# A four-layer trunk on one core: the seven block products stepped singly, their first weight blocks loaded a block ahead, and x scaled on VectorE

## The chip, the core and the metric

The kernel runs on one core of a Trainium2 chip. The metric is the time of one execution in microseconds on the device; smaller is better. Three runs of the kernel before gave 1944.89, 1944.83 and 1941.6 us, median 1944.83. Engines are named as in the profile: PE is TensorE, with PEld for its weight loads, DVE is VectorE, ACT is ScalarE, POOL is GpSimd, and SP is the SyncE queue that issues nearly all DMAs.

## What is computed

```python
for i in range(4):                    # x is (1, 256, 1024) float32, D_FF = 2816
    x = x + 0.5 * swiglu(rms_norm(x, g[i,0]), gate[i,0], up[i,0], down[i,0])
    hn = rms_norm(x, g[i,1])
    x = x + (short_conv, mla, spatial_gating)[i % 3](hn)
    x = x + 0.5 * swiglu(rms_norm(x, g[i,2]), gate[i,1], up[i,1], down[i,1])

def swiglu(x, w_gate, w_up, w_down):
    return (silu(x @ w_gate) * (x @ w_up)) @ w_down
```

So there are twelve blocks in a row: feed-forward, mixer, feed-forward, four times over, all in float32. The 256 rows of x are two tiles of 128 rows.

## The kernel before

**Products.** A float32 operand is split into a high part of a rounded type (`whi`, made by ACT, line 111) and the rest (`wlo`, made by DVE, line 117). Each product is three matmuls: high by high (L327), high by low (L328), low by high (L330). The weights come in units of 512 KB: SP loads one into a `raw` buffer, ACT and DVE split it, PE uses it for both tiles. `Weights.get` makes up to AHEAD = 4 units ahead of the one in use; N_RAW = 5 raw buffers bound how far the loads run ahead.

**Turns.** The program is written out in one order, by two generators, one per tile. `advance(t)` takes a tile one turn further, which is usually six matmuls, and then runs what `later(n, ...)` has put off by n turns. Tile 0 leads by LAG = 4 turns; in a feed-forward block it is closed up to 1 turn (`follow`). Every engine executes its own instructions in this order, so an instruction that waits holds all that stand behind it on its engine.

**The seven products.** In each feed-forward block but the first, columns 2048 to 2559 of gate and of up are computed by Winograd's form of the 2x2 block product: the two tiles' rows and the two halves of the inner dimension are the blocks, and seven products of 128x512 by 512x256 replace eight. `sevens` is a third generator, the lane. Its first four half-steps make the sums s1 to s4 of the left blocks (`combine`, L603, on DVE; `high`, L608, on ACT; `low`, L613, on DVE), then come the right blocks' first form and, for each of two times seven products, a half-step that prepares and one that issues twelve matmuls (L744). `beside` grants the lane RATE = 0.6 half-steps a turn. Its credit grows from the turn on which the lane is set up, half-steps are taken only when all four halves of x are ready as left operands (`lhs`), and the `while` then takes as many as the credit covers. The four weight blocks of the gate unit (512 KB each, five buffers) are loaded when the lane is set up.

**x between blocks.** When half an x tile (512 columns) has its residual added (L418 or L420, DVE), `prepare_x` turns it over for the next block. Ahead of a feed-forward block with seven products it is `evened` first: ACT multiplies it by the last row scale (L436). Then either PE transposes it (L293), or DVE transposes 32x32 blocks (L455) and a DMA write (`xturn`, L461) and four reads (L465) do the rest, with raw loads held back between write and read. X_TAKE turns after the residual, ACT applies the gains (`take`, L441) and the half is split into high (L285, ACT) and low (L286, DVE).

Of the kernel before, what the change touches and what calls it, by code (L numbers as in the profile page):

```python
# [13 lines left out]
F32 = mybir.dt.float32  # L14
# [3 lines left out]
AF = mybir.ActivationFunctionType  # L18
# [22 lines left out]
N_UNITS = 9  # L41
N_RAW = 5
N_SEVENS_RAW = 5
N_SLOTS = 27
N_BIG = 4
# [116 lines left out]
def program(nc, pools, order, x, positions, norm_g, ffn_gate, ffn_up, ffn_down,  # L162
# [192 lines left out]
    def rows_into_x(t, a, m, ks, tail, factor, then):  # L355

        ps = [acc(), acc()]
        cols = [slice(0, 512), slice(512, 1024)]  # L360
        for n, k in enumerate(ks[: len(ks) - tail]):
            products(ps, a(k), k % 4, unit(t, m, k, 1, 0, D), 0, cols, n == 0, False)
            yield
        for h in range(2):
            for n in range(len(ks) - tail, len(ks), 2):
                k = ks[n]
                w = unit(t, m, k, 2, 512 * h, 512)
                for j in range(2):
                    products([ps[h]], a(k + j), (k + j) % 4, w, j, [cols[0]], n + j == 0, n + j == len(ks) - 1)
                if n < len(ks) - 2:  # L370
                    yield
            residual(t, ps[h], h, factor)
            if then is not None:
                prepare_x(t, h, *then)
            else:
                (nc.sync, nc.scalar)[h].dma_start(out=out[0, t * P : (t + 1) * P, 512 * h : 512 * h + 512], in_=x_half(t, h))
            if h == 0:
                yield
        in_chain[t] = True
# [45 lines left out]

    def prepare_x(t, h, i, which, halves_by_dma, evened):

# [3 lines left out]
        lhs[t][h] = None  # L431
        src = [x_half(t, h)]

        def even():
            src[0] = slot([P, 512])
            nc.scalar.activation(src[0], x_half(t, h), AF.Copy, scale=scales[t][0])  # L436

# [7 lines left out]
        if evened:  # L445
            even()
        if halves_by_dma[h]:
            later(evened, lambda: turn_half(src[0], take, X_TAKE - evened))
        else:
            later(X_TURN + evened, lambda: turn_by_pe(t, h, g, src[0]))  # L450

# [48 lines left out]
    def ffn(t, i, j, shared, then):  # L500
# [5 lines left out]
        if t == NT - 1 and seven:  # L506
            lanes.append(sevens(i, j, seven, shared))
        gate, up, down = (("gate", i, j), ("up", i, j), ("down", i, j))
# [31 lines left out]
        def body():  # L540
            yield from linear_group(t, a, [(gate, 0, lambda ps: gate_done(0, ps)), (up, 0, lambda ps: up_done(0, ps)),
                                           (gate, 512, lambda ps: gate_done(1, ps))], 512, NK)
            for n in plain[1:]:
# [4 lines left out]
                up_done(n, (yield from linear(t, a, up, c, w, NK)))  # L548
                yield
            yield from rows_into_x(t, lambda k: hs[k // 4], down, ks, tail, 0.5, then)  # L550

# [28 lines left out]

    def sevens(i, j, chunks, shared):

        (a11, a12), (a21, a22) = lhs[0], lhs[1]
        units = [(m, FF_CHUNKS[n][0]) for n in chunks for m in ("gate", "up")]
        raws = [{} for _ in units]

        def load(u, name_):
            if u == len(units):
                return
            m, c0 = units[u]  # L590
            row, col = int(name_[0]) - 1, int(name_[1]) - 1
            view = matrices[m][i, j].rearrange("(kt p) n -> p kt n", p=P)[:, 4 * row : 4 * row + 4, c0 + 256 * col : c0 + 256 * col + 256]
            raws[u][name_] = sevens_pool.tile([P, 4, 256], F32, tag="block", name=name("block"))
            nc.sync.dma_start(out=raws[u][name_], in_=view)

        for block in ("11", "12", "22", "21"):
            load(0, block)

# [108 lines left out]
        for s in range(last + 1):  # L707
# [4 lines left out]
            sum_of(s + 2)  # L712
            if (s + 1) % 7 == 4:
                load(u + 1, "12")
            if (s + 1) % 7 == 5:
                load(u + 1, "22")
                load(u + 1, "21")
            if q == 1:
                load(u + 1, "11")
            if pending:  # L720
# [39 lines left out]
    def conv(t, i, ia, shared, then):  # L760
# [44 lines left out]
        parts = ((c_done, D), (h_done, 2 * D), (b_done, 0))  # L805
        yield from linear_group(t, a, [(w_in, c, lambda ps, f=f: f(0, ps)) for f, c in parts], 512, NK)
        for f, c in parts:
            f(1, (yield from linear(t, a, w_in, c + 512, 512, NK)))
            yield
        yield from rows_into_x(t, lambda k: ms[k // 4], ("conv_out", ia), range(NK), OUT_TAIL, 1.0, then)  # L810


    sg_wT = [fixed([P, 4, P], f"sg_wT{j}") for j in range(2)]
    sg_gain = []

    def prepare_spatial(ic):
# [15 lines left out]
        def turn_over(j, wm):  # L832
            tr = transposed([wm[:, k, :] for k in range(4)])
            nc.scalar.activation(sg_wT[j], tr, AF.Copy)

        later(70, load)

    def spatial(t, i, ic, _, then):
# [47 lines left out]

        w_in = ("sg_in", ic)
        yield from linear_group(t, a, [(w_in, D, v_done), (w_in, D + 512, v_done), (w_in, 0, lambda ps: u_done(0, ps))], 512, NK)
        u_done(1, (yield from linear(t, a, w_in, 512, 512, NK)))
# [131 lines left out]
    def mla(t, i, ib, shared, then):  # L1021
# [164 lines left out]
        def finish(b8, o):  # L1186
            os_[b8] = lhs_of(o.rearrange("p h d -> p (h d)"), 4)

        for h0 in range(0, HEADS, per):
            p = scores(h0)  # L1190
# [47 lines left out]

    def beside():
        credit[0] += RATE  # L1240
        while lanes and credit[0] >= 1 and all(half_ is not None for tile_ in lhs for half_ in tile_):
            credit[0] -= 1
# [39 lines left out]
```

## Time and profile before

| | |
|---|---|
| profiled execution, its own time | 1946.05 us |
| its span | 1944.3 us |
| median of three runs | 1944.83 us |
| busy: PE, DVE, ACT, POOL | 95%, 66%, 52%, 7% of the span |
| mean granted TensorE clock | 0.978 |
| DMA | 400.36 MB, mean 206 GB/s |

Busy time of PE covers the time in which at least one matmul is in flight. The granted clock is 1.00 at TensorE's upper level, 2.4 GHz, and 0.50 at the lower, 1.2 GHz; in a stretch at 0.50 PE is busy and yet does half the work. The seven lanes start near 319, 516, 814, 1009, 1285, 1480 and 1772 us of the span.

### The profile page before, as it was taken

Reading aid. Unit: us, or ns where it says so; the run is one execution under the profiler, and the core shown is the slowest. Engines: PE = TensorE matmul, PEld = TensorE weight load, DVE = VectorE, ACT = ScalarE, POOL = GpSimd, SP = SyncE. Lnnn points to the kernel's source line nnn. Section 1 sums busy time; section 2 is a strip of 40 time slices with the busy share of each in tenths; the row PEclk is TensorE's granted clock in tenths of the full one; section 3 lists DMA queues with packets and bytes.
Section 4 is the critical chain, followed back from the end, with each engine's and each line's share of the span. In section 5 each row is a group of like instructions: output and inputs, shape, how many; then the busy total and the mean of one; then the engine's idle time right before and its main releaser. Section 6 shows DMA issues by size and latency. Waiting matters only on the chain.

```text
span 1944.3 us, 24911 instructions
## 1 busy us (share of the span) xinstructions
PE 1854.1 (95%) x9022; PEld 1535.9 (79%) x9022; DVE 1280.7 (66%) x1560; ACT 1009.3 (52%) x1447; POOL 131.9 (7%) x263
## 2 busy tenths in 40 slices
PE   8999998999799979899989998989998999998999
PEld 7888787887688868688868886868876887787887
DVE  5565677765577576686658664677656765667763
ACT  5344545545554485554455445565455544545542
POOL 2000101000600140100010101100000000000000
PEclk9999998999899999999999999989998999998999
DMA  7687656687667841666876786566876687656684
GB/s 242 225 238 223 211 177 213 196 239 221 196 211 216 241 131 43 207 206 200 240 231 205 219 242 203 155 202 202 240 229 206 200 246 212 199 187 200 196 255 134
DMA packets 251611, 400.36 MB, mean 206 GB/s; under 512 B 25414, under 2 KB 116448, under 8 KB 251488
## 3 DMA queue, kind: packets, MB, share of 16 engines
q1 hardware_dynamic: 250480, 397.09, 66.6%
q0 software_dynamic: 608, 1.11, 0.3%
q8 instruction: 70, 1.15, 0.2%
q10 hardware_dynamic: 400, 0.57, 0.1%
q14 instruction: 53, 0.43, 0.1%
HBM read 365.67 MB, written 33.03 MB: 205 GB/s over the span
## 4 chain that ended last, share of the span: by engine, by line
PE 46%; DVE 5%; DMA 5%; ACT 4%; issue 2%; SPq 1%; ACTq 0%; DVEq 0%
PE acc L327 13%; PE acc L328 13%; PE acc L330 13%; PE acc L744 5%; DMA xturn<-s 2%; DVE wlo L117 2%; ACT whi L111 1%; DMA raw<-in_ffn_gate_dram 1%; PE tr L293 1%; ACT s L441 1%; SPq L465 1%; DVE s L603 1%; ACT s L608 1%; PE acc L1176 1%; PE acc L1149 1%
## 5 line engine op out<-in xcount | busy, mean ns | idle before, releaser
L328 PE MATMUL acc<-wlo,s 128*128 128x512 f32 (+2 forms) x2440 | 939.2, 385 | 42.0 <-DVE wlo L117 42.0
L327 PE MATMUL acc<-whi,s 128*128 128x512 f32 (+2 forms) x2440 | 944.2, 387 | 22.6 <-ACT s L285 19.5
L330 PE MATMUL acc<-whi,s 128*128 128x512 f32 (+2 forms) x2440 | 903.3, 385 | 0.0
L117 DVE TENSOR_TENSOR wlo<-raw,whi 128x1024 fp32r<-128x1024 f32 (+1 forms) x578 | 686.3, 1212 | 159.5 <-ACT whi L111 157.3
L111 ACT ACTIVATE whi<-raw 128x1024 fp32r<-128x1024 f32 (+1 forms) x578 | 588.8, 1048 | 193.0 <-DMA raw<-in_ffn_down_dram 103.5
L328 PEld LDWEIGHTS acc<-wlo,s 128*128 128x128 f32 x2440 | 462.9, 190 | 135.7 <-DVE wlo L117 46.8
L327 PEld LDWEIGHTS acc<-whi,s 128*128 128x128 f32 x2440 | 462.5, 190 | 119.0 <-ACT s L285 26.3
L330 PEld LDWEIGHTS acc<-whi,s 128*128 128x128 f32 x2440 | 462.6, 190 | 102.7 <-DVE s L286 6.4
L744 PE MATMUL acc<-whi,s 128*128 128x256 f32 x784 | 162.7, 290 | 0.0
L608 ACT ACTIVATE whi<-block 128x1024 fp32r<-128x1024 f32 x98 | 103.4, 1055 | 111.3 <-DVE block L640 111.3
L744 PEld LDWEIGHTS acc<-whi,s 128*128 128x128 f32 x784 | 134.0, 198 | 4.7
L613 DVE TENSOR_TENSOR wlo<-block,whi 128x1024 fp32r<-128x1024 f32 x98 | 118.7, 1212 | 23.1 <-ACT whi L608 22.7
L520 ACT ACTIVATE s<-acc,evened 128x512 f32<-128x512 f32 (+1 forms) x70 | 45.0, 644 | 163.7 <-PE acc L330 163.7
L744 PE MATMUL acc<-wlo,s 128*128 128x256 f32 x392 | 115.0, 293 | 7.7 <-DVE wlo L613 7.7
L529 DVE SCALAR_TENSOR_TENSOR s<-acc,evened,s 128x512 f32<-128x512 f32 (+1 forms) x70 | 48.5, 693 | 90.9 <-PE acc L330 90.9
L405 POOL TENSOR_TENSOR total<-ss,ss 128x1 f32<-128x1 f32 x26 | 14.9, 574 | 1363.3 <-ACT s L396 1363.3
L286 DVE TENSOR_TENSOR s<-s,s 128x512 fp32r<-128x512 f32 (+1 forms) x58 | 39.8, 687 | 97.5 <-ACT s L285 97.5
L744 PEld LDWEIGHTS acc<-wlo,s 128*128 128x128 f32 x392 | 77.4, 197 | 15.3 <-DVE wlo L613 11.3
L420 DVE SCALAR_TENSOR_TENSOR x<-acc,x 128x512 f32<-128x512 f32 x32 | 22.1, 691 | 93.2 <-PE acc L330 93.2
L319 DVE TENSOR_TENSOR s<-big,s 128x512 fp32r<-128x512 f32 x68 | 46.0, 676 | 41.6 <-ACT s L318 38.7
L640 DVE TENSOR_TENSOR block<-block,block 128x1024 f32<-128x1024 f32 x56 | 68.4, 1221 | 1.0
L436 ACT ACTIVATE s<-x,rstd 128x512 f32<-128x512 f32 x28 | 20.3, 724 | 81.4 <-DVE x L420 47.7
(151 smaller groups left out, 900.7 us busy)
## 6 DMA issues: line engine op xcount, KB each, us to landing
raw<-in_ffn_down_dram SPq DMA_DIRECT2D x176, 512.0 KB, 6.0
raw<-in_ffn_gate_dram SPq DMA_DIRECT2D x148, 512.0 KB, 4.1
raw<-in_ffn_up_dram SPq DMA_DIRECT2D x148, 512.0 KB, 4.6
raw<-in_conv_w_in_dram SPq DMA_DIRECT2D x48, 512.0 KB, 4.7
turn<-big SPq DMA_DIRECT2D x32, 512.0 KB, 4.0
big<-turn SPq DMA_DIRECT2D x128, 128.0 KB, 7.0
block<-in_ffn_gate_dram SPq DMA_DIRECT2D x28, 512.0 KB, 9.6
block<-in_ffn_up_dram SPq DMA_DIRECT2D x28, 512.0 KB, 6.5
```

Source lines behind the costliest of these rows:

```text
L111: self.nc.scalar.activation(hi, self.loaded[u], AF.Copy)
L117: self.nc.vector.tensor_tensor(out=lo, in0=src, in1=hi.bitcast(F32), op=ALU.subtract)
L319: nc.vector.tensor_tensor(out=lo.rearrange("p k (i b) -> p k i b", b=32), in0=src, in1=hi.bitcast(F32).rearrange("p k (i b) -> p k i b", b ...
L327: nc.tensor.matmul(ps, lhsT=ah[:, k, :], rhs=wh[:, wk, c], start=first, stop=False)
L328: nc.tensor.matmul(ps, lhsT=ah[:, k, :], rhs=wl[:, wk, c], start=False, stop=False)
L330: nc.tensor.matmul(ps, lhsT=al[:, k, :], rhs=wh[:, wk, c], start=False, stop=last)
L520: nc.scalar.activation(sg[n], ps[:, :w], AF.Silu, scale=r)
L529: nc.vector.scalar_tensor_tensor(out=h, in0=ps[:, :w], scalar=r, in1=sg[n], op0=ALU.mult, op1=ALU.mult)
L608: nc.scalar.activation(hi, src, AF.Copy)
L613: nc.vector.tensor_tensor(out=lo, in0=src, in1=hi.bitcast(F32), op=ALU.subtract)
L640: nc.vector.tensor_tensor(out=to, in0=to, in1=raws[u][added[q]], op=ALU.add)
L744: nc.tensor.matmul(ps[:, :256], lhsT=f[:, k, :], rhs=w[:, k, :], start=q in (0, 1, 3) and k + n == 0, stop=k == 3 and n == 2, skip_group_c ...
```

## The change

Six edits go together.

1. `beside` lets credit grow only while all four halves of x are ready, and takes at most one half-step in a turn.
2. The four gate blocks of the seven products are loaded by `load_first`, some turns apart, in the block ahead: in the mixer for the feed-forward block behind it, and in the down product of a layer's second feed-forward block for the next layer's first. The up blocks are loaded two and two at the half-steps of products 4 and 5, in four buffers in place of five.
3. `prepare_x` scales x with a `tensor_scalar` on DVE (L443) where ACT did it (L436), and the transposition follows on the same turn where it came one later.
4. `take` of the first half (h = 0) comes 10 turns after the residual where it came 12, behind a feed-forward block with seven products.
5. N_RAW is 6, N_SEVENS_RAW is 4.
6. N_SLOTS is 29; two constant tiles of the spatial mixer become slots.

```diff
-N_RAW = 5
-N_SEVENS_RAW = 5
-N_SLOTS = 27
+N_RAW = 6
+N_SEVENS_RAW = 4
+N_SLOTS = 29
...
             if then is not None:
-                prepare_x(t, h, *then)
+                prepare_x(t, h, min(X_TAKE, tail) if tail > OUT_TAIL and not h else X_TAKE, *then)
...
-            nc.scalar.activation(src[0], x_half(t, h), AF.Copy, scale=scales[t][0])
...
         if evened:
-            even()
+            src = slot([P, 512])
+            nc.vector.tensor_scalar(src, x_half(t, h), scales[t][0], None, op0=ALU.mult)
         if halves_by_dma[h]:
-            later(evened, lambda: turn_half(src[0], take, X_TAKE - evened))
+            turn_half(src, take, turns)
         else:
-            later(X_TURN + evened, lambda: turn_by_pe(t, h, g, src[0]))
+            later(X_TURN, lambda: turn_by_pe(t, h, g, src))
...
+            if t == 0 and j == 1 and i + 1 < DEPTH:
+                load_first(i + 1, 0, 6)
             yield from rows_into_x(t, lambda k: hs[k // 4], down, ks, tail, 0.5, then)
...
+    def block_of(i, j, n, m, name_):
+        row, col = int(name_[0]) - 1, int(name_[1]) - 1
+        c0 = FF_CHUNKS[n][0] + 256 * col
+        view = matrices[m][i, j].rearrange("(kt p) n -> p kt n", p=P)[:, 4 * row : 4 * row + 4, c0 : c0 + 256]
+        raw = sevens_pool.tile([P, 4, 256], F32, tag="block", name=name("block"))
+        nc.sync.dma_start(out=raw, in_=view)
+        return raw
+
+    def load_first(i, j, every):
+        raws = blocks_of[i, j] = {}
+        for n, block in enumerate(("11", "12", "22", "21")):
+            def load(block=block):
+                raws[block] = block_of(i, j, SEVENS[0], "gate", block)
+
+            later(1 + every * n, load)
...
-            if (s + 1) % 7 == 4:
-                load(u + 1, "12")
-            if (s + 1) % 7 == 5:
-                load(u + 1, "22")
-                load(u + 1, "21")
-            if q == 1:
-                load(u + 1, "11")
+            if q == 4:
+                load(u + 1, "11", "12")
+            if q == 5:
+                load(u + 1, "22", "21")
...
     def beside():
+        if not all(half_ is not None for tile_ in lhs for half_ in tile_):
+            return
         credit[0] += RATE
-        while lanes and credit[0] >= 1 and all(half_ is not None for tile_ in lhs for half_ in tile_):
+        if credit[0] >= 1:
             credit[0] -= 1
```

On DVE at the start of the seven products in the feed-forward block whose lane starts near 516 us, before: L286 is the low part of the last half of x, L603 the four sums, L613 their low parts, L117 the low parts of weight units 166 and 167, and the last row the first block's low part.

```order
L286 TENSOR_TENSOR s_570_4438<-s_568_4432,s_569_4437 128x512
L603 TENSOR_TENSOR s_575_4449<-s_553_4307,s_568_4432 128x512
L613 TENSOR_TENSOR s_577_4452<-s_575_4449,s_576_4451 128x512
L603 TENSOR_TENSOR s_578_4455<-s_575_4449,s_531_4222 128x512
L613 TENSOR_TENSOR s_580_4458<-s_578_4455,s_579_4457 128x512
L603 TENSOR_TENSOR s_581_4461<-s_531_4222,s_553_4307 128x512
L613 TENSOR_TENSOR s_583_4464<-s_581_4461,s_582_4463 128x512
L603 TENSOR_TENSOR s_584_4467<-s_564_4352,s_578_4455 128x512
L117 TENSOR_TENSOR wlo166_4422<-raw166_4331,whi166_4421 128x1024
L613 TENSOR_TENSOR s_586_4470<-s_584_4467,s_585_4469 128x512
L117 TENSOR_TENSOR wlo167_4486<-raw167_4375,whi167_4485 128x1024
L613 TENSOR_TENSOR wlo_588_4483<-block_571_4441,whi_587_4482 128x1024
```

The same place in the changed kernel, where the sums are L615 and their low parts L625:

```order
L286 TENSOR_TENSOR s_572_4446<-s_570_4440,s_571_4445 128x512
L117 TENSOR_TENSOR wlo166_4430<-raw166_4300,whi166_4429 128x1024
L615 TENSOR_TENSOR s_573_4458<-s_545_4290,s_570_4440 128x512
L117 TENSOR_TENSOR wlo167_4464<-raw167_4339,whi167_4463 128x1024
L625 TENSOR_TENSOR s_575_4461<-s_573_4458,s_574_4460 128x512
L615 TENSOR_TENSOR s_576_4482<-s_573_4458,s_521_4196 128x512
L526 SCALAR_TENSOR_TENSOR s_580_4497<-acc_543_4261,evened_541_4258,s_569_4438 128x512
L528 STREAM_TRANSPOSE big_579_4496<-s_580_4497 128x4x4x32
L117 TENSOR_TENSOR wlo168_4488<-raw168_4383,whi168_4487 128x1024
L625 TENSOR_TENSOR s_578_4485<-s_576_4482,s_577_4484 128x512
L615 TENSOR_TENSOR s_581_4510<-s_521_4196,s_545_4290 128x512
L625 TENSOR_TENSOR s_583_4513<-s_581_4510,s_582_4512 128x512
```

Unit 166's low part stood behind seven rows of sums and now stands ahead of all of them. The first block's low part follows seventeen rows behind L286, eleven before; in all seven blocks the first of the lane's matmuls stands 42 matmuls later on PE.

On ACT where the first half of x is taken for the same block, before: L436 scales, L396 sums squares, L441 and L285 take and split the first half of tile 0.

```order
L111 ACTIVATE whi157_4171<-raw157_4058 128x1024
L111 ACTIVATE whi158_4188<-raw158_4090 128x1024
L436 ACTIVATE s_518_4198<-x0_83,rstd_302_2542 128x512
L396 ACTIVATE s_524_4207,ss_523_4206<-x0_83 128x512
L441 ACTIVATE s_531_4222<-s_500_4088,columns0_90 128x128 x4
L285 ACTIVATE s_532_4227<-s_531_4222 128x512
```

In the changed kernel, where the take is L437:

```order
L111 ACTIVATE whi157_4180<-raw157_4048 128x1024
L437 ACTIVATE s_521_4196<-s_503_4093,columns0_90 128x128 x4
L285 ACTIVATE s_522_4201<-s_521_4196 128x512
L111 ACTIVATE whi158_4211<-raw158_4066 128x1024
L396 ACTIVATE s_536_4228,ss_535_4227<-x0_83 128x512
```

The take moved ahead of weight unit 158 and of the rows that wait for the second half's residual. On SP, the four gate blocks of this lane stood in one run behind raw170 before:

```order
L100 DMA raw169_4395<-in_ffn_up_dram 128x2x512
L100 DMA raw170_4413<-in_ffn_up_dram 128x2x512
L594 DMA block_571_4441<-in_ffn_gate_dram 128x4x256
L594 DMA block_572_4443<-in_ffn_gate_dram 128x4x256
L594 DMA block_573_4445<-in_ffn_gate_dram 128x4x256
L594 DMA block_574_4447<-in_ffn_gate_dram 128x4x256
L100 DMA raw171_4473<-in_ffn_up_dram 128x2x512
```

In the changed kernel they stand apart among the down weights of the block ahead (the second of them here):

```order
L100 DMA raw145_3796<-in_ffn_down_dram 128x1024
L100 DMA raw146_3808<-in_ffn_down_dram 128x2x512
L588 DMA block_476_3819<-in_ffn_gate_dram 128x4x256
L100 DMA raw147_3822<-in_ffn_down_dram 128x2x512
L100 DMA raw148_3834<-in_ffn_down_dram 128x2x512
```

All four moved, ahead by 17 to 28 raw loads.

## Rows read from the trace of the kernel before

**Rows 1.** The page, busy time and share of each engine.
```profile
PE 1854.1 (95%) x9022; PEld 1535.9 (79%) x9022; DVE 1280.7 (66%) x1560; ACT 1009.3 (52%) x1447; POOL 131.9 (7%) x263
```
**Rows 2.** PE's waits: releaser, us in total, times, longest us.
```profile
PE acc L328 <- DVE wlo L117: 42.0, 12, 6.5
PE acc L327 <- ACT s L285: 19.5, 15, 4.4
PE acc L744 <- DVE wlo L613: 7.7, 7, 1.1
```
**Rows 3.** Stretches at the seven lane starts: us, PE busy, clock, DMA share, GB/s.
```profile
319.00:333.00 14.00, 8.39 (x27) 0.63 0.50 150
...
1771.00:1787.00 16.00, 9.31 (x30) 0.68 0.56 172
sum 101.50, PE 54.87; mean PE 7.84
```
**Rows 4.** PE in the seven stretches of lowered clock behind those starts.
```profile
322.05:332.25 10.20, 7.61 (x23) 0.50 0.38 107
...
sum 71.40, PE 47.76; mean PE 6.82
```
**Rows 5.** DVE in order of time at one start: start us, us.
```profile
811.23 0.69 DVE L286 TENSOR_TENSOR s<-s,s 128x512 fp32r<-128x512 f32 x1 [5.68 <-ACT s L285]
811.84 0.68 DVE L603 TENSOR_TENSOR s<-s,s 128x512 f32<-128x512 f32 x1
813.22 0.69 DVE L613 TENSOR_TENSOR s<-s,s 128x512 fp32r<-128x512 f32 x1 [0.70 <-ACT s L608]
...
818.41 1.22 DVE L117 TENSOR_TENSOR wlo<-raw,whi 128x1024 fp32r<-128x1024 f32 x1
819.54 0.69 DVE L613 TENSOR_TENSOR s<-s,s 128x512 fp32r<-128x512 f32 x1
```
**Rows 6.** A down product and a mixer: PE, PEld, DVE, ACT, POOL, clock, DMA share, GB/s.
```profile
1120.00:1160.00 40.00, 40.00 (x179) 32.42 (x178) 23.12 (x28) 19.23 (x27) 0.00 (x0) 1.00 0.95 261
1230.00:1270.00 40.00, 40.00 (x187) 32.64 (x187) 25.07 (x29) 21.07 (x34) 4.36 (x9) 1.00 0.57 175
```
**Rows 7.** ACT in order of time where a first half is taken.
```profile
481.43 0.72 ACT L436 ACTIVATE s<-x,rstd 128x512 f32<-128x512 f32 x1 [0.95 <-DVE x L420]
...
482.67 1.27 ACT L441 ACTIVATE s<-s,columns 128x128 f32<-128x128 f32 x4
483.97 0.63 ACT L285 ACTIVATE s<-s 128x512 fp32r<-128x512 f32 x1
```
**Rows 8.** PE's waits from 470 to 500 us, then from 1170 to 1195 us.
```profile
PE acc L327 <- ACT s L285: 2.4, 2, 1.2
PE acc L327 <- ACT s L285: 1.2, 2, 0.6
```
**Rows 9.** ACT in order of time where the spatial mixer starts.
```profile
1201.33 1.06 ACT L111 ACTIVATE whi<-raw 128x1024 fp32r<-128x1024 f32 x1 [6.25 <-DMA raw<-in_sg_w_in_dram]
```
**Rows 10.** PE in the lowered clock behind that wait; columns as in rows 3.
```profile
1206.10:1212.90 6.80, 5.87 (x14) 0.50 0.53 166
```
**Rows 11.** Durations by form: busy us, mean ns, idle before.
```profile
L117 DVE TENSOR_TENSOR wlo<-raw,whi 128x1024 fp32r<-128x1024 f32 x570 | 678.7, 1216 | 158.0 <-ACT whi L111 155.9 <-DMA raw<-in_ffn_up_dram 1.7
L436 ACT ACTIVATE s<-x,rstd 128x512 f32<-128x512 f32 x28 | 20.3, 724 | 81.4 <-DVE x L420 47.7 <-DVE x L418 33.7
L603 DVE TENSOR_TENSOR s<-s,s 128x512 f32<-128x512 f32 x28 | 19.4, 691 | 0.0
L776 DVE TENSOR_SCALAR s<-s,columns 128x128 f32<-128x128 f32 x32 | 9.0, 283 | 7.0 <-ACT s L771 7.0
```
**Rows 12.** DVE in a stretch of the lane's products; then clock, DMA share, GB/s.
```profile
830.00:900.00 70.00, 52.27 (x54) 1.00 0.61 190
```
**Rows 13.** Block loads: count, KB, median us to landing.
```profile
block<-in_ffn_gate_dram SPq DMA_DIRECT2D x28, 512.0 KB, 9.6
block<-in_ffn_up_dram SPq DMA_DIRECT2D x28, 512.0 KB, 6.5
```
**Rows 14.** Line 594: landing of all block loads.
```profile
DMA to landing us min/median/max: 4.7/7.9/11.5
```

More of the change, by code (lines that the diff above doesn't have):

```diff
@@ L424, in gain_at, with prepare_x @@
         return columns[0][:, g0 : g0 + 4]
-    def prepare_x(t, h, i, which, halves_by_dma, evened):
+    def prepare_x(t, h, turns, i, which, halves_by_dma, evened):
         g = gain_at(i, which, h)
         lhs[t][h] = None
-        src = [x_half(t, h)]
-        def even():
-            src[0] = slot([P, 512])
-            nc.scalar.activation(src[0], x_half(t, h), AF.Copy, scale=scales[t][0])
+        src = x_half(t, h)
         def take(y):
@@ L506, in ffn @@
         if t == NT - 1 and seven:
-            lanes.append(sevens(i, j, seven, shared))
+            lanes.append(sevens(i, j, seven, shared, blocks_of[i, j]))
         gate, up, down = (("gate", i, j), ("up", i, j), ("down", i, j))
@@ L579, in follow, with sevens, load @@
         lag[0] = turns
-    def sevens(i, j, chunks, shared):
-        (a11, a12), (a21, a22) = lhs[0], lhs[1]
[L584 to L597, printed above, removed]
+    blocks_of = {}
+    def block_of(i, j, n, m, name_):
[11 more added lines that the diff above has]
+            later(1 + every * n, load)
+    def sevens(i, j, chunks, shared, first):
+        (a11, a12), (a21, a22) = lhs[0], lhs[1]
+        units = [(n, m) for n in chunks for m in ("gate", "up")]
+        raws = [first] + [{} for _ in units[1:]]
+        def load(u, *names):
+            for name_ in names:
+                if u < len(units):
+                    raws[u][name_] = block_of(i, j, *units[u], name_)
         forms = {}
@@ L806, in conv @@
         yield from linear_group(t, a, [(w_in, c, lambda ps, f=f: f(0, ps)) for f, c in parts], 512, NK)
+        if t == 0:
+            load_first(i, 1, 6)
         for f, c in parts:
@@ L810, in conv @@
         yield from rows_into_x(t, lambda k: ms[k // 4], ("conv_out", ia), range(NK), OUT_TAIL, 1.0, then)
-    sg_wT = [fixed([P, 4, P], f"sg_wT{j}") for j in range(2)]
+    sg_wT = [None] * 2
     sg_gain = []
@@ L833, in turn_over @@
             tr = transposed([wm[:, k, :] for k in range(4)])
+            sg_wT[j] = slot([P, 4, P])
             nc.scalar.activation(sg_wT[j], tr, AF.Copy)
@@ L887, in spatial @@
         w_in = ("sg_in", ic)
+        if t == 0:
+            later(16, lambda: load_first(i, 1, 5))
         yield from linear_group(t, a, [(w_in, D, v_done), (w_in, D + 512, v_done), (w_in, 0, lambda ps: u_done(0, ps))], 512, NK)
@@ L1187, in finish @@
             os_[b8] = lhs_of(o.rearrange("p h d -> p (h d)"), 4)
+        if t == 0:
+            load_first(i, 1, 4)
         for h0 in range(0, HEADS, per):
```

## The prediction, made before the changed kernel ran

> **What bounds the kernel now.** I read the page's busy shares first, then PE's waits, then the clock around the long ones, then the other engines in order of time there. PE is busy for 95% of the span [rows 1], so the time is PE's work, plus what PE waits, plus what a lowered clock costs. The waits are few [rows 2]: 42.0 us for DVE's low weight parts, 19.5 us for the high part of x, 7.7 us for the first low part of the lane. They are bunched. In the seven stretches in which a lane starts, 101.50 us long together, PE is busy for 54.87 us [rows 3], so 46.6 us are idle: seven waits of 1.1 us for the lane's own low part (7.7) and seven waits of 38.9 us together, 5.6 us each, in the row of 42.0.
>
> Behind each of the seven the clock is at 0.50, TensorE's 1.2 GHz level, for 10.2 us: 71.40 us in all, of which PE is busy for 47.76 [rows 4]. At 2.4 GHz that work takes half, so 23.9 us are lost there.
>
> Why PE waits is seen on DVE [rows 5]. From 811.84 us it makes the four sums and three of their low parts, each low part 0.70 us after ACT's high part, and only at 818.41 comes the weight unit that PE waits for. The credit that had grown while x was not ready pays out four half-steps at once. DVE is held here by its own order, not by a transfer.
>
> **The change part by part**, against the profiled execution's 1946.05 us.
>
> *The burst.* Unit 166's low part now stands directly behind the last half of x, so PE's 5.6 us wait has no cause left: all four sums and their low parts go between later units, spread over some seven turns. Taken: minus 38.9 us. What is late next is the lane's first low part. From L286 on DVE has 18 instructions until that is done: five of 128x1024, nine of 128x512, two products with the gate and two transposes. By the distance from start to start in the burst (0.61 us for 128x512, 1.13 for 128x1024 [rows 5]; I put 0.7 on the other four), this is 5.5 + 5.7 + 2.8 = 14.0 us, and 0.7 for one low part that still stands right behind its sum. PE has nine turns of six matmuls, 54, until it needs it; at 40.00 us for 179 [rows 6], 0.22 us each, 12.1 us. DVE can begin before PE does if x is ready early. So the lane's own wait lies between none and some 3 us a start, and I leave it at its present 1.1 us: 0, with ends of minus 7.7 and plus 13.
>
> *The clock.* Without the long wait I expect no stretch at 0.50 at the seven starts: minus 23.9 us, with an end of 0.
>
> *The earlier take.* The first half's take stands behind the second half's scaling and squares [rows 7], and PE waits 1.2 us for its high part, twice at each of three changes from feed-forward to feed-forward and 0.6 us twice at each of two changes into a mixer [rows 8]: 3 x 2.4 + 2 x 1.2 = 9.6 us. It moves 2 turns ahead, 2 x 6 x 0.22 = 2.6 us, past the rows that held it. Minus 9.6, with an end of 0 if the transfer has then not landed.
>
> *The sixth raw unit.* The wait of 4.4 us in the row of 19.5 comes where ACT sits 6.25 us before a raw unit [rows 9] and then does the mixer's first results ahead of x's high part. A load one unit earlier is one unit of two turns earlier, 2.6 us. Behind it lie 5.87 us at 0.50 [rows 10], 2.9 us lost. Between 0 and minus 7.3; I take minus 4, near the 2.6 us with part of the clock.
>
> *Scaling on DVE.* 28 times DVE multiplies 128x512 by a column. ACT's 0.72 us [rows 11] goes, and with it the hand-over in which DVE waited for ACT. The form is not in the trace; the nearest rows are 0.283 us for a quarter of the width and 0.691 us for two full inputs, so 28 times 0.28 to 0.69 us. I take 0.69, the same width: 19 us more on DVE, four at each of seven changes of block, where PE works on the other tile's last turns. PE's transposes of a scaled half come one turn sooner and may wait for it. Plus 2 us, between 0 and plus 19.
>
> The Trainium skill, in VectorE: DVE Perf Modes, section The perf-mode tier table, says that a float32 tensor_scalar from SBUF runs at twice the rate of a tensor_tensor; its figures would make this about 0.42 us, an estimate, and the 19 us then 12. No row here shows it at this width. [...]
>
> *Block loads.* 4 x 524,288 bytes a lane leave the start, where they stood ahead of raw units, for places where the DMA share is 0.57 in a mixer and 0.95 in a down product [rows 6]. Cover: four units made ahead, 4 x 2.6 = 10.6 us, and one more raw buffer. 0 here; the price without cover is the last rival. The slots and the two moved constants: 0.
>
> Sum: -38.9 - 23.9 + 0 - 9.6 - 4 + 2 = -74.4, so 1946.05 - 74.4 = 1871.7. The median of the runs before is 1.2 us under the profiled one: **1870 us**.
>
> **Rivals.**
>
> *The start stall shrinks but stays long enough.* By whole durations (1.22 and 0.69 us [rows 11]) DVE's 18 instructions are 15.2 us, with the 0.7 us 15.9, against PE's 12.1: a wait of 3.8 us at each lane's first product, 2.7 more than now, and the clock at 0.50 as today. Then -74.4 + 18.9 + 23.9 = -31.6: 1913 us. For it: DVE is at 75% in the lane [rows 12] and every weight unit passes through it. Against: start to start is shorter than a duration, and DVE begins ahead of PE when x is early. 0.13.
>
> *The up blocks come late.* They are asked for three half-steps before use; a half-step is 1.67 turns of 1.3 us and half of the twelve narrow matmuls, some 3 us, so 9 us. Landing takes 6.5 us in the median but up to 11.5 [rows 13, 14]: ACT could stand 2.5 us at each, with weight units behind it. If PE feels all of it, 7 x 2.5 = 17.5: 1888 us. Against: units made ahead. 0.06.
>
> *The time is handed on.* If DVE bounds the whole lane, the saved waits come back later in it: 1945 us. Against: DVE is idle a quarter of it [rows 12], and PE's waits there are none. 0.02.
>
> *Slower: the moved block loads starve PE.* 2.1 MB at 261 GB/s are 8.0 us of a DMA system that in the down product is at 0.95 [rows 6]. If the cover doesn't hold, PE waits 8 us in the block ahead and loses another 3.4 us of clock, as now (23.9 / 7): 11.4 us seven times is 80, and the sum is 5 us above before, 1950 us. It decides from 74.4 / 7 = 10.6 us a block. For it: ACT already waits for raw units in down products. Against: only three of the seven loads lie in a down product, and PE is busy through all 40 us of it [rows 6]. 0.04.
>
> **How the numbers follow.** The forecast's own range is 1852 (all ends of gain: -87.4, and the 5.5 us of other waits for L285, which is 19.5 - 9.6 - 4.4) to 1887 (the scaling at plus 19), chance 0.75. With the rival of late blocks that is 0.81 at most; since my terms may err together I go toward the first rival, up to 1905. Faster holds the forecast, the first two rivals: 0.94; handed on: within 0.2%, 0.02; slower 0.04. Those 0.2%, some 4 us, are about what a measurement of this kernel can tell from no change.
>
> **What would show it.** PE's row for L328 waiting on L117 falls from 42.0 to a few us; at the seven starts the clock stays at 1.00 and its mean rises from 0.978 to above 0.985; L327's waits on L285 fall to some 8 us in 5; the lane's own wait stays near 7 times 1.1. It is wrong if a wait of several us stays at the starts with 0.50 behind it, if ACT's waits for raw down units (or blocks) pass on to PE, or if PE's transposes wait for L443.

## The result and the profile after

The changed kernel takes **1865.8 us** (median of four runs, 1864.4 to 1868.16) against 1943.82 us for the kernel before in the same session: ratio 0.9601, 95% interval 0.9585 to 0.9618. The forecast was 1870 us, with a range of 1852 to 1905. The profiled execution took 1866.14 us, with a span of 1864.4 us and a granted clock of 0.993.

First the page's busy row of the changed kernel, to be held against [rows 1].

```profile
PE 1830.7 (98%) x9022; PEld 1525.3 (82%) x9022; DVE 1290.3 (69%) x1588; ACT 986.5 (53%) x1419; POOL 136.5 (7%) x263
```

With the same 9022 matmuls PE is busy 23.4 us less, in the main because fewer of them run at the lower clock, and its idle time (span minus busy) falls from 1944.3 - 1854.1 = 90.2 to 1864.4 - 1830.7 = 33.7 us. These two differences, 23.4 and 56.5, are the whole 79.9 us. PE's waits after, as in [rows 2] (L753 is the lane's matmul, L625 and L620 its low and high parts; L744, L613 and L608 before):

```profile
PE acc L753 <- DVE wlo L625: 10.7, 7, 1.7
...
PE acc L328 <- DVE wlo L117: 3.0, 5, 0.8
...
PE acc L753 <- ACT whi L620: 1.5, 3, 0.7
PE acc L327 <- ACT s L285: 1.3, 1, 1.3
```

The waits for weight units went from 42.0 to 3.0, those for the high part of x from 19.5 to 1.3, and the lane's own wait rose from 7.7 to 12.2 (10.7 + 1.5). The 1.3 that is left lies in the MLA mixer. Now the lane starts, as in [rows 3] (us, PE busy, clock, DMA share, GB/s):

```profile
318.00:332.00 14.00, 12.70 (x61) 1.00 0.40 112
...
792.00:806.00 14.00, 11.66 (x51) 0.93 0.42 129
...
sum 100.00, PE 87.81; mean PE 12.54
```

12.2 us are idle in these seven stretches, where 46.6 were. What is left of the lowered clock at the starts are three stretches of 3.4 us (the stretches of [rows 4] were 10.2 us and seven):

```profile
803.93:807.35 3.42, 2.83 (x12) 0.53 0.15 58
513.80:517.21 3.41, 3.41 (x15) 0.53 0.00 0
1251.30:1254.70 3.40, 3.40 (x10) 0.50 0.00 0
sum 10.23, PE 9.64; mean PE 3.21
```

Away from the starts, the stretch behind the spatial mixer's wait [rows 10] is gone. But in the MLA mixer three stretches at 0.50, 13.65 us together, lie between 681 and 719 us, where the kernel before had one of 3.4 us, at 738 us.

DVE in order of time at the start that [rows 5] showed (start us, us; in brackets the idle time before and what ended it):

```profile
787.64 0.69 DVE L286 TENSOR_TENSOR s<-s,s 128x512 fp32r<-128x512 f32 x1 [7.92 <-ACT s L285]
788.25 1.22 DVE L117 TENSOR_TENSOR wlo<-raw,whi 128x1024 fp32r<-128x1024 f32 x1
789.38 0.69 DVE L615 TENSOR_TENSOR s<-s,s 128x512 f32<-128x512 f32 x1
791.71 1.22 DVE L117 TENSOR_TENSOR wlo<-raw,whi 128x1024 fp32r<-128x1024 f32 x1 [1.65 <-ACT whi L111]
...
803.29 1.18 DVE L625 TENSOR_TENSOR wlo<-block,whi 128x1024 fp32r<-128x1024 f32 x1
```

The weight unit now stands directly behind x's last half and the sums lie between the units. The block's low part, the last of the ramp, is done 16.8 us after the ramp begins (804.47 - 787.64); PE came 1.68 us too early for it here.

### The profile page after: what moved, and what is told of

The parts are those of the page before. It is cut to its first block, busy times and chain, and to the rows that moved or that the text cites. A ratio compares the mean times of both kernels' runs of the same rounds, so it can differ in the third digit from the quotient of the medians.

```text
span 1864.4 us, 24887 instructions
## 1 busy us (share of the span) xinstructions
PE 1830.7 (98%) x9022; PEld 1525.3 (82%) x9022; DVE 1290.3 (69%) x1588; ACT 986.5 (53%) x1419; POOL 136.5 (7%) x263
## 4 chain that ended last, share of the span: by engine, by line
PE 55%; DVE 4%; ACT 2%; issue 1%; DMA 1%; SPq 0%; DVEq 0%; ACTq 0%
PE acc L328 16%; PE acc L327 16%; PE acc L330 16%; PE acc L753 5%; DVE wlo L117 1%; PE tr L293 1%; ACT whi L111 1%; PE acc L1190 1%; DMA xturn<-s 1%; PE acc L1163 1%; DVE s L615 0%; DVE s L625 0%; ACT s L620 0%; ACT s L437 0%; DVE wlo L625 0%
## 5 line engine op out<-in xcount | busy, mean ns | idle before, releaser
L328 PE MATMUL acc<-wlo,s 128*128 128x512 f32 (+2 forms) x2440 | 933.9, 383 | 3.0 <-DVE wlo L117 3.0
L117 DVE TENSOR_TENSOR wlo<-raw,whi 128x1024 fp32r<-128x1024 f32 (+1 forms) x578 | 685.7, 1212 | 117.9 <-ACT whi L111 115.8
L330 PEld LDWEIGHTS acc<-whi,s 128*128 128x128 f32 x2440 | 459.7, 188 | 97.1 <-DVE s L286 1.0
L327 PEld LDWEIGHTS acc<-whi,s 128*128 128x128 f32 x2440 | 460.0, 189 | 95.5 <-ACT whi L111 2.9
L328 PEld LDWEIGHTS acc<-wlo,s 128*128 128x128 f32 x2440 | 460.3, 189 | 93.9 <-DVE wlo L117 4.7
L620 ACT ACTIVATE whi<-block 128x1024 fp32r<-128x1024 f32 x98 | 103.5, 1056 | 126.9 <-DVE block L652 126.9
L753 PE MATMUL acc<-whi,s 128*128 128x256 f32 x784 | 157.3, 283 | 1.5 <-ACT whi L620 1.5
L753 PEld LDWEIGHTS acc<-whi,s 128*128 128x128 f32 x784 | 128.2, 190 | 6.6 <-ACT whi L620 3.0
L625 DVE TENSOR_TENSOR wlo<-block,whi 128x1024 fp32r<-128x1024 f32 x98 | 118.5, 1209 | 15.0 <-ACT whi L620 15.0
L753 PE MATMUL acc<-wlo,s 128*128 128x256 f32 x392 | 111.7, 285 | 10.7 <-DVE wlo L625 10.7
L286 DVE TENSOR_TENSOR s<-s,s 128x512 fp32r<-128x512 f32 (+1 forms) x58 | 39.9, 688 | 112.7 <-ACT s L285 111.2
L405 POOL TENSOR_TENSOR total<-ss,ss 128x1 f32<-128x1 f32 x26 | 8.7, 335 | 1318.7 <-ACT s L396 1318.7
L396 ACT ACTIVATE s<-x 128x512 bf16<-128x512 f32 x48 | 30.2, 630 | 137.5 <-DVE x L420 99.7
L753 PEld LDWEIGHTS acc<-wlo,s 128*128 128x128 f32 x392 | 74.6, 190 | 15.9 <-DVE wlo L625 12.5
```

The lines of the kernel that those rows point to most:

```text
L117: self.nc.vector.tensor_tensor(out=lo, in0=src, in1=hi.bitcast(F32), op=ALU.subtract)
L327: nc.tensor.matmul(ps, lhsT=ah[:, k, :], rhs=wh[:, wk, c], start=first, stop=False)
L328: nc.tensor.matmul(ps, lhsT=ah[:, k, :], rhs=wl[:, wk, c], start=False, stop=False)
L330: nc.tensor.matmul(ps, lhsT=al[:, k, :], rhs=wh[:, wk, c], start=False, stop=last)
L620: nc.scalar.activation(hi, src, AF.Copy)
L625: nc.vector.tensor_tensor(out=lo, in0=src, in1=hi.bitcast(F32), op=ALU.subtract)
```

## The experiments

All times are medians, ratios are to the kernel before in the same session. Differences from the changed kernel are taken from ratios, times 1943.8 us; with intervals of 0.003 in width such a difference is uncertain by some 4 us. "PE idle" is span minus PE busy. PE busy and idle are read in one execution of each kernel; with five raw units this took 1890.4 us and with the sixth raw unit alone 1931.67 us, 4.7 and 4.9 us above their medians.

| kernel | us | ratio, 95% interval | PE busy | PE idle |
|---|---|---|---|---|
| before | 1943.82 | 1 | 1854.1 | 90.2 |
| changed | 1865.8 | 0.9601, 0.9585 to 0.9618 | 1830.7 | 33.7 |
| burst back | 1916.48 | 0.9857, 0.9842 to 0.9872 | 1850.5 | 65.0 |
| single half-steps alone, on before | 1905.28 | 0.9797, 0.9779 to 0.9815 | 1846.4 | 59.0 |
| blocks loaded at the start | 1863.42 | 0.9583, 0.9568 to 0.9597 | 1828.6 | 33.3 |
| before, waits filled | 1940.52 | 0.9983, 0.9966 to 0.9999 | 1878.2 | 59.4 |
| late take | 1876.1 | 0.9647, 0.9626 to 0.9667 | 1831.3 | 42.8 |
| five raw units | 1885.72 | 0.9689, 0.967 to 0.9707 | 1842.6 | 46.1 |
| five raw, five block buffers | 1883.05 | 0.9699, 0.9678 to 0.972 | 1834.8 | 45.4 |
| five raw, blocks at the start | 1884.1 | 0.97, 0.9683 to 0.9716 | 1834.8 | 44.7 |
| sixth raw alone, on before | 1926.8 | 0.9922, 0.9907 to 0.9937 | 1858.0 | 72.0 |
| scaling on ScalarE | 1868.55 | 0.9605, 0.9588 to 0.9623 | 1829.2 | 35.9 |
| first block ahead of the sums | 1854.06 | 0.9532, 0.9518 to 0.9546 | 1824.7 | 27.1 |
| the same, blocks at the start | 1899.74 | 0.9775, 0.976 to 0.9789 | 1844.9 | 53.7 |

**The burst, undone in the changed kernel.**

```diff
     def beside():
-        if not all(half_ is not None for tile_ in lhs for half_ in tile_):
-            return
         credit[0] += RATE
-        if credit[0] >= 1:
+        while lanes and credit[0] >= 1 and all(half_ is not None for tile_ in lhs for half_ in tile_):
```

> The changed kernel with one thing undone: half-steps whose credit has piled up are again paid all at once when x is complete. Block loads, early take, six raw units and the scaling on VectorE stay. Theory (the burst of several half-steps made the wait, and the wait brought the clock down): PE's row for L328 waiting on wlo of L117 goes from 3.0 us back to about 40, the granted clock falls to 0.50 behind each lane start, and the time rises by about 60 us (38.9 of waits + 23.9 of clock), 1925 to 1930 us. Rival (it was the loads at the lane's start, in front of raw units): no more than 5 us, 1866 to 1871.

Plus 49.8 us. PE's waits of this kernel, the row in question:

```profile
PE acc L328 <- DVE wlo L117: 36.3, 16, 5.5
```

33.3 of the us are the wait that returned, and PE's busy time grows by 19.8 us with the clock. The mechanism holds, the rival of the loads falls. But it is 50 and not 60: four of the seven waits are now only 3.9 to 4.1 us, where they were 4.5 to 6.5 before.

**Single half-steps, alone in the kernel before.**

```diff
     def beside():
+        if not all(half_ is not None for tile_ in lhs for half_ in tile_):
+            return
         credit[0] += RATE
-        while lanes and credit[0] >= 1 and all(half_ is not None for tile_ in lhs for half_ in tile_):
+        if credit[0] >= 1:
```

> The kernel before with one thing done: a half-step at a time, never several at once. All else is as before, the first block's loads at the lane's start too. Theory (the burst alone): minus 63 us, 1880 to 1885 us, with the waits on L117 at lane starts down to a few us and the clock at 1.00 there. Rival (the lane's first loads stand ahead of raw units and make the wait): less than 15 us gained, above 1929. Between the two: if the first blocks, loaded late, now hold ACT and so PE, about 4 us at each of seven starts come back, some 1910.

Minus 39.5 us, so the theory's number is missed by some 23. PE's waits of this kernel:

```profile
PE acc L327 <- ACT s L285: 17.7, 14, 4.9
PE acc L744 <- DVE wlo L613: 11.8, 7, 1.8
PE acc L744 <- ACT whi L608: 7.7, 7, 2.0
...
PE acc L328 <- DVE wlo L117: 2.7, 4, 0.8
```

The time lies nearest to the case between the two, but its reason is not borne out: ACT waits for no block in this trace. The long wait did go, 42.0 to 2.7, but 11.8 us came back as the lane's waits for its block (19.5 against 7.7). Two in a row, up to 3.7 us, still bring the clock down, as in this stretch (us, PE busy, clock, DMA share, GB/s):

```profile
811.50:821.00 9.50, 6.00 (x21) 0.64 0.27 87
```

Six of the seven starts still have a stretch at 0.50, of 3.4 or 6.8 us. Together:

```profile
sum 27.31, PE 23.48; mean PE 3.91
```

Half of that busy time, 11.7 us, is still lost there, of 23.9 before, and over the whole kernel PE's busy time falls by only 7.7 us (1854.1 - 1846.4), where all six edits give 23.4. The other edits must have more to do with the starts than the forecast gave them.

**The early block loads, undone.** `load_first` loads nothing, and the lane loads its four gate blocks at its start.

```diff
-                raws[block] = block_of(i, j, SEVENS[0], "gate", block)
+                pass
...
+        load(0, "11", "12", "22", "21")
```

> The changed kernel with the four gate blocks of each lane loaded at the lane's start, as before, and not during the block ahead. Theory (the blocks are used some half-steps after the start, and landing takes 6 to 10 us): from nothing to 1 us at each of seven starts, 1866 to 1873 us. Rival (the early loads carry a good part of the gain): each lane's first product waits 3 us or more, and the clock falls behind it at 3.4 us each, so plus 45, about 1910.

Minus 3.5 us, with intervals that overlap: no loss. In this order of work the early loads bring nothing that can be measured.

**The waits of the kernel before, filled with work.**

```diff
+    def fill():
+        ps = acc()
+        for _ in range(FILL):
+            nc.tensor.matmul(ps, lhsT=ident_r, rhs=ident_r.unsqueeze(1).broadcast_to([P, 4, P]), start=True, stop=True)
+        later(6, lambda: nc.vector.tensor_copy(out=tiny(1, "fill", 2), in_=ps[:, :1]))
...
+        if lanes and credit[0] >= 2 and all(half_ is not None for tile_ in lhs for half_ in tile_):
+            later(FILL_AT, fill)
```

> The kernel before with 24 matmuls of 128x512 on a constant added at each of seven lane starts, just ahead of the unit that PE waits for; VectorE reads one column of their result six turns later. They take about 5.2 us of PE each time, in a wait of 5.6. Nothing else is changed, and the result of these matmuls goes nowhere. Theory (the clock falls because PE stands idle, not because DVE or the loads are busy): the granted clock stays at 1.00 behind the starts, and the 23.9 us lost there are gained although work is added: about 1920 us. Rival 1 (the fall of the clock belongs to the lane's start itself): the clock still falls there, and the time is 1944 or a few us above. Rival 2 (the added matmuls stand in PE's way, in part before or after the wait): up to 7 x 5.2 = 36 us above the 1920, so 1920 to 1956 with the clock at 1.00.

Ratio 0.9983: 168 matmuls more and no slower. PE in order of time at one start; the filler is L1243, and all other lines are one higher than before:

```profile
808.82 5.62 PE L1243 MATMUL acc<-ident_r 128*128 128x512 f32 x24
814.27 0.40 PE L328 MATMUL acc<-whi,s 128*128 128x512 f32 x1
815.50 0.51 PE L329 MATMUL acc<-wlo,s 128*128 128x512 f32 x1 [0.83 <-DVE wlo L118]
...
819.32 0.58 PE L745 MATMUL acc<-wlo,s 128*128 128x256 f32 x1 [2.27 <-DVE wlo L614]
```

The filler takes 814.27 - 808.82 = 5.45 us, 38.2 in seven. Idle time falls by 30.8 us, and the busy time without the filler is 1878.2 - 38.2 = 1840.0, which is 14.1 us below the 1854.1 before: -30.8 - 14.1 + 38.2 gives the span's -6.7. DVE's burst and the loads are as they were, so the lowered clock followed PE's idleness, not the lane's start. The full 23.9 did not come, since the lane's own wait grew to 2.27 us at five of the seven starts and the clock fell behind each of these five, for 3.4 or 6.8 us where it had been 10.2. And the filler, 38.2 us, is longer than the waits that it took: PE's row for weight units went from 42.0 to 6.8, so 35.2. The time lies where rival 2 put it, but the mean clock (0.991 in this execution, 0.985 to 0.993 in all ten) is short of its 1.00.

**The take, undone.**

```diff
-                prepare_x(t, h, min(X_TAKE, tail) if tail > OUT_TAIL and not h else X_TAKE, *then)
+                prepare_x(t, h, X_TAKE, *then)
```

> The changed kernel with one thing undone: the first half of x is taken two turns later again. Theory A (the early take is worth its own waits and no more): PE waits for ACT's high part of x 1.2 us six times and 0.6 us four times, 9.6 us, and the time is about 1875 us. Theory B, drawn from the run that changed the half-steps alone (waits at the seven lane starts of 1.7 to 3.7 us, 19 us in all, with 0.50 behind them, against 12 in the changed kernel): the later take also moves the lane's first sums and blocks back by some 2 us, so that each lane start waits about 1 us more and the clock falls behind most of them: 9.6 + 7 + some 12 us of clock, about 1893 us. Rival (a late take is hidden): 1866.

Plus 8.9 us, the size of theory A. PE's waits show why it is not dearer:

```profile
PE acc L753 <- DVE wlo L625: 10.3, 7, 1.7
PE acc L327 <- ACT s L285: 7.2, 11, 1.3
...
PE acc L327 <- ACT whi L111: 4.3, 3, 2.3
```

Ten waits of 0.6 us come back, 5.9 us (7.2 - 1.3), half of the 1.2 at the feed-forwards before, and so less than the 9.6 of theory A. Another 2.6 us stand in PE's row for the high parts of weight units (1.7 in the changed kernel), which the theory did not have. The lane's row does not grow: theory B falls.

**Five raw units in place of six.** `N_RAW = 5`, nothing else.

> The changed kernel with five raw units in place of six, the rest as it is. Theory (the sixth lets the weights of the mixer with sg_w come one unit sooner): the wait of 4 to 5 us for ACT's high part at the start of that mixer comes back, with some 3 us of lowered clock behind it: 1870 to 1874 us. Rival 1 (the early take alone has moved that wait away): 1866. Rival 2 (the block loads of the lanes need the room): ACT waits for raw units in down products and PE for ACT, several times 1 to 3 us, above 1880.

Plus 17.1 us, four times the forecast's term; of the rivals the second comes nearest, though its place is another. PE's waits, then ACT in order of time before one of them:

```profile
PE acc L327 <- ACT s L285: 10.8, 6, 4.0
PE acc L753 <- ACT whi L620: 3.6, 5, 1.7
```

```profile
499.55 1.06 ACT L111 ACTIVATE whi<-raw 128x1024 fp32r<-128x1024 f32 x1 [6.20 <-DMA raw<-in_ffn_gate_dram]
...
501.09 1.26 ACT L437 ACTIVATE s<-s,columns 128x128 f32<-128x128 f32 x4
502.38 0.63 ACT L285 ACTIVATE s<-s 128x512 fp32r<-128x512 f32 x1
```

ACT stands 6.20 us in front of a raw gate unit, and x's last take and high part stand behind it: the pattern of [rows 9], but at feed-forward blocks. It was there to be read in ACT's waits for raw units in the kernel before:

```profile
ACT whi L111 <- DMA raw<-in_ffn_down_dram: 103.5, 79, 3.1
...
ACT whi L111 <- DMA raw<-in_ffn_gate_dram: 27.7, 8, 5.3
ACT whi L111 <- DMA raw<-in_conv_w_in_dram: 15.8, 7, 6.6
ACT whi L111 <- DMA raw<-in_sg_w_in_dram: 6.5, 2, 6.3
```

In the changed kernel the first of the four is left, and 1.6 us in all of others:

```profile
ACT whi L111 <- DMA raw<-in_ffn_down_dram: 73.3, 44, 4.9
```

Three kernels ask whether the sixth unit is worth this by itself. **Both buffer counts as before** (`N_RAW = 5`, `N_SEVENS_RAW = 5`):

> The changed kernel with the exchange of buffers undone in full: five raw units and five block buffers, as before (the run with five raw units had four block buffers). Theory (the sixth raw unit alone was worth the 20 us seen there): 1883 to 1888 us, PE's waits for ACT's high part of x near 10 us in 5 or 6. Rival (the fifth block buffer makes up for a part, because block loads no longer wait for one another): the first product's waits for the block's high part fall from 3.6 us to 1.5, and the time to 1875 to 1881 us.

Plus 19.0 us: the fifth block buffer makes up for nothing. **Five raw units, with the block loads back at the lane's start:**

> The changed kernel with five raw units, and with the four gate blocks loaded at the lane's start. With the blocks loaded in the block ahead, five raw units cost 20 us (1885.7 against 1865.8). Theory A (the sixth raw unit is the cover of the moved block loads: they stand on the queue ahead of raw units, and without it ACT gets those 6 us late): with the loads back at the lane's start, the waits for ACT's high part of x at 503, 983 and 1441 us go, only the one of 4 us at the start of the mixer with sg_w stays, and the time is 1868 to 1874 us. Theory B (raw units are short whatever the blocks do): all these waits stay and the time is 1882 to 1888 us.

Plus 19.2 us on the changed kernel, and 22.7 on the one that has six raw units and the same loads (0.97 against 0.9583). That is theory B: it is not the moved block loads that need the cover. The waits of 1.9 and 1.8 us for x at 503 and 1441 are gone in PE's list, but others stand for them:

```profile
PE acc L755 <- DVE wlo L627: 11.1, 7, 1.7
PE acc L755 <- ACT whi L622: 6.8, 5, 1.9
PE acc L327 <- ACT s L285: 6.5, 4, 3.9
```

The first product now waits 6.8 us for its block's high part. With six raw units and the same loads that row is:

```profile
PE acc L755 <- ACT whi L622: 1.3, 2, 0.7
```

ACT still waits 28.4 us for raw gate units, up to 5.8 at once, and x's last take still stands behind the wait; PE now meets the delay later, at the block's high part with which ACT's work at the lane start ends. The run with single half-steps alone has the same two rows, 7.7 us of PE's waits for that high part and 29.9 us of ACT's waits for raw gate units. That it lost its time through them is likely, but no run joins single half-steps and the sixth raw unit alone. **The exchange alone in the kernel before** (`N_RAW = 6`, `N_SEVENS_RAW = 4`):

> The kernel before with the exchange of buffers alone: six raw units and four block buffers, all else as it was. The prediction priced it at minus 4 us. Theory A (the sixth covers the moved block loads above all, and these are not moved here): the 4.4 us of wait at the start of the mixer with sg_w and the clock behind it go, minus 4 to 8, 1936 to 1940 us. Theory B (raw units were short before as well): minus 15 to 20, 1924 to 1929 us, with PE's row for L285 down from 19.5 to about 10. Rival (four block buffers hold the lanes): no gain or slower, 1944 or above.

Ratio 0.9922, minus 15.2 us: theory B. PE's waits, against [rows 2]:

```profile
PE acc L328 <- DVE wlo L117: 32.9, 12, 5.2
PE acc L327 <- ACT s L285: 10.9, 11, 1.3
```

8.6 us less for x, and 9.1 less at the lane starts: part of what the forecast gave to the burst was ACT's lateness in front of it. The clock does not gain here (PE busy 1858.0): waits of 3.9 to 5.2 us are still there at all seven starts, each with 10.2 us at 0.50 behind it.

**Scaling on ScalarE, on the same turn.**

```diff
-            nc.vector.tensor_scalar(src, x_half(t, h), scales[t][0], None, op0=ALU.mult)
+            nc.scalar.activation(src, x_half(t, h), AF.Copy, scale=scales[t][0])
```

> The changed kernel with x scaled by ScalarE on the same turn, not by VectorE. ScalarE's form took 0.724 us in the kernel before, VectorE's 0.487 us in the changed one. Theory (the edit is near nothing): 28 times 0.24 us later, partly hidden, plus 0 to 5, 1866 to 1871 us. Rival 1 (VectorE is the fuller engine, and its 13.6 us are worth more on ScalarE): 5 us and more below, under 1861. Rival 2 (the hand-over between the engines was a main part of the waits for x): PE's waits on the high part of x rise from 1.3 us to 10 and more, with lowered clock behind them, 1880 and above.

Plus 0.8 us, no difference that can be told. PE's transposes wait a little for it, and that is all:

```profile
PE tr L293 <- ACT s L443: 2.4, 5, 0.6
```

**One step more: the first block's parts ahead of the sums.** The changed kernel's last lane wait is for the block's low part, which DVE makes at the end of the ramp.

```diff
+        high(0, raws[0]["11"], w_pool, [P, 4, 256])
         s1 = combine(a21[2], a22[2], ALU.subtract)
         high("s1", s1, None, [P, 4, P])
         yield
+        low(0)
         low("s1")
...
-        high_of(0)
         yield
-        low(0)
```

> The changed kernel with one step more: the high and low part of the lane's first weight block are made in the lane's first two half-steps, ahead of the sums of x, and not behind them. Theory (the lane's first product waits for the block's low part because VectorE makes it last): PE's waits on the block parts go from 12.2 us (10.7 + 1.5) to under 3, and the three stretches at 0.50 behind them go, 12 + 3 x 1.7 = 17 us at most: 1849 to 1856 us. Rival 1 (the wait passes to the next product, whose left part is a sum and is now 2.3 us later): 1860 to 1866. Rival 2 (VectorE's work in the two half-steps now holds the raw units' low parts in front of PE): waits on L117 rise above 10 us, 1870 and more.

**1854.06 us**, ratio 0.9532: minus 13.4 against the changed kernel, within the theory's 1849 to 1856, and the fastest of all the kernels here. PE's waits, the seven starts as above, and DVE at one:

```profile
PE acc L328 <- DVE wlo L117: 5.1, 9, 0.8
...
PE acc L753 <- DVE wlo L625: 0.9, 2, 0.5
```

```profile
792.00:806.00 14.00, 13.51 (x70) 1.00 0.31 95
...
sum 100.00, PE 98.03; mean PE 14.00
```

```profile
788.41 1.22 DVE L117 TENSOR_TENSOR wlo<-raw,whi 128x1024 fp32r<-128x1024 f32 x1 [1.65 <-ACT whi L111]
789.56 1.22 DVE L625 TENSOR_TENSOR wlo<-block,whi 128x1024 fp32r<-128x1024 f32 x1
```

The block's low part (789.56) lies in the second half-step, DVE catches up before the first sum is needed, and the clock is 1.00 in each of the seven stretches. **The same with the gate blocks loaded at the lane's start:**

> The version with the first block's parts made ahead of the sums (1854.06 us), with the four gate blocks loaded at the lane's start and not in the block ahead. Landing of block loads took 4.8 us at the least, 7.1 in the median and 10.6 at most in the changed kernel. Theory (this order has need of the early loads: the block's high part is now the lane's first work on ScalarE, and stands there until the block has landed): ScalarE is held 5 to 10 us at each lane start, behind it the raw units' high parts, and PE for 2 to 5 us seven times with lowered clock: 1875 to 1910 us. Rival (ScalarE has the room, the block lands while x is turned): within 3 us of 1854.

1899.74 us, plus 47.2 against the version above. ACT's wait in this kernel, and its first work at one start:

```profile
ACT whi L622 <- DMA block<-in_ffn_gate_dram: 56.7, 7, 9.3
```

```profile
805.94 1.06 ACT L622 ACTIVATE whi<-block 128x1024 fp32r<-128x1024 f32 x1 [8.43 <-DMA block<-in_ffn_gate_dram]
```

Here the early loads are worth 47 us; in the changed kernel's own order they were worth nothing.

## Why the prediction was right, and which term was mis-sized

*The sum.* The forecast was 74.4 us; the profiled executions gave 79.9 (1946.05 - 1866.14).

*Burst and clock* (38.9 + 23.9 = 62.8). The waits are met to the figure, 39.0 us in PE's row for L328. The clock is not: of the 23.9 us lost at the starts half of PE's 9.64 us in the lowered clock, 4.8, is still lost, so 19.1 came back. That PE's busy time fell by 23.4 is no proof of the term, for it is the whole kernel's, with the 2.9 us behind the spatial mixer's wait that the forecast gave to the raw unit. And the burst is not the only cause of either. Undone, it costs 49.8; alone on the kernel before it is worth 39.5. Some 9 us of the waits belonged to late raw units, as the exchange alone showed. And with single half-steps alone, shorter waits kept about half of the lowered clock at the starts.

*The lane's first low part* (0, between -7.7 and +13). It is +4.5, 12.2 against 7.7. The ramp was sized at 14.7 us and took 16.8 at the start shown: DVE waited 1.65 and 0.24 us for ACT's high parts of units, besides the 0.7.

*The earlier take* (-9.6). Undone it costs 8.9, but only 5.9 of this in the row that the forecast named. Which of the other edits took the rest of that row's 9.6 away is not shown.

*The sixth raw unit* (-4, between 0 and -7.3). This is the step that failed: it measured 15.2 us alone on the kernel before and 17.1 to 19.2 in the three undone versions (22.7 where the blocks load at the start in both kernels), beyond the end that I gave. I priced the one wait of 4.4 us at the spatial mixer by "a load one unit earlier is 2.6 us". ACT's waits for raw gate, conv and mixer units were 50.0 us in 17 in the rows above, up to 6.6 us each; the unit alone leaves 5.0 of them in the exchange's trace and so removes the rest, with the waits of PE that followed from them and the clock behind those. Of the 5.5 us of other waits for L285 that stood only in my range, 4.2 were of this kind: the exchange alone took 8.6 us from that row, 4.4 of them the wait that I had priced. I had left some 8 us in the row, and 1.3 stayed.

*Scaling* (+2, between 0 and +19). 0.8 us undone, below what can be told. The form that no row of before had:

```profile
L443 DVE TENSOR_SCALAR s<-x,rstd 128x512 f32<-128x512 f32 x28 | 13.6, 487 | 1.0
```

0.487 us, not the 0.69 I took. The estimate from the Trainium skill's page VectorE: DVE Perf Modes, section The perf-mode tier table, was 0.42 us; the measurement lies nearer to it. The Trainium skill's page Perfetto Trace Analysis, section Optimizing Scalar/DVE Operations, says that moving work from DVE to ScalarE may make sense if DVE is saturated. DVE was not, at 69% of the span against ScalarE's 53%, and moving these 28 instructions back made no difference that can be told.

*Block loads* (0). Confirmed, 3.5 us the other way within the uncertainty.

*The total* was right because two errors met, and that they nearly cancelled was luck: the burst was over-priced by 13 us (62.8 against 49.8) and the sixth unit under-priced by 11 to 15. Undone one by one, the parts come to 49.8 + 8.9 + 19.0 + 0.8 - 3.5 = 75.0 of 77.6 (0.0399 x 1943.8). No run undoes the transposition one turn sooner, the new places of the up blocks or the slots, so these are not priced by themselves.

*The rivals.* None came. The first (3.8 us at each start, with the clock) lies nearest: 12.2 us in seven, and the clock falls behind three. The up blocks and the starved down products show in no wait of PE.

## What to carry to other kernels

When a buffer is added, price it from the whole list of waits of the engine that reads it, each with what stands behind it in that engine's order; here the one wait of PE that I took for the whole priced it at 4 us, and it was worth 15. The list is not the price itself: 50.0 us of ACT's waits stood in it. A sum that comes out does not confirm its terms: only undoing each part showed that two were wrong by nearly the same amount. And where a wait moves to the last item of a ramp, ask first whether that item can be made first; that was 13 us for two lines moved, but only because its load had been made early.

## What the runs showed of the hardware that was not expected

The clock was touched by shorter waits than the 5.6 us of the kernel before. In the changed kernel the four starts with a last wait of 1.68 or 1.75 us were followed by 3.4 us near 0.50 in three cases, the three with 1.30 to 1.33 us in none. This gives no limit between the two. In the MLA mixer of the same execution a wait of 1.31 us, 2 us behind another of 1.03, was followed by 3.4 us at 0.50 (PE's wait, then the stretch):

```profile
680.52 0.50 PE L327 MATMUL acc<-whi,s 128*128 128x512 f32 x1 [1.31 <-ACT s L285]
```

```profile
681.27:684.68 3.41, 3.41 (x12) 0.50 0.33 126
```

And in the run with the blocks loaded at the start the second lane's wait, 1.78 us where it was 1.75, left the clock at 1.00 (from 509 to 519 us).

A `tensor_scalar` of 128x512 in float32 took 0.487 us on VectorE, where a `tensor_tensor` of that size took 0.69.
